# Spreading the odd layer's query products over more steps, and issuing a step's sums and normalising ahead of the next step's maxima

## The chip, the core and the metric

One core of one Trainium2 chip runs the whole program once. The metric is the device time of that launch in microseconds, the median of the runs. TensorE (PE) multiplies, ScalarE (ACT) evaluates functions and copies, VectorE (DVE) and GpSimd (POOL) do elementwise work, and SyncE (SP) issues the large loads. Each engine works through its own instructions in the order in which they were issued, and a semaphore holds an instruction until what it needs is there.

## The reference

Two layers of a diffusion trunk run over 128 context tokens and 256 latent tokens. Each layer is half a SwiGLU block, a mixer, and another half SwiGLU block. The change lies in the mixers, and mostly in that of the odd layer: windowed attention with 16 query heads, 4 key heads and one sink logit per head.

```
q = rms_norm(h @ wq); k = rms_norm(h @ wk); v = h @ wv      # q, k rotated for latent tokens
context rows:  p = softmax([q k_ctx^T, sink])               # 128 keys
latent rows:   p = softmax([q k_cache^T, q k_latent^T masked to +-128, sink])   # 384 keys
o = p[..., :-1] @ v;  out = o @ w_out
```

The even layer's mixer (differential attention beside a short convolution) runs through the same pipeline function.

## The kernel before

Activations lie transposed: 128 channels on the partitions, 384 tokens along the free axis. Every fp32 product of a weight chunk is done as three products of high and low parts (L178, L179, L180). A projection of 128 output channels is eight row chunks of three such products, summed in one PSUM tile named proj.

Tile pools give out buffers, but the order of instructions is the order in which the Python code issues them. In the odd layer odd_mixer projects keys, values and the first four heads' queries (u = 0), and then runs an attention pipeline of 24 steps. A step is a pair of heads (u, c) and one of three blocks of 128 rows: block 0 is the context rows with 128 keys, blocks 1 and 2 are latent rows with 384 keys. So steps 0, 3, 6 and so on are short, and the other two of every three are long. Below, step s is the s-th of them and block 0, 1 or 2 its kind.

The function pipeline issues, for loop counter s: a(s), the scores on PE (L1208, L1215), the maxima on DVE (L1221, L1223, L1225, L1229) and the exponentials on ACT (L1233, then L1237 for the sink); m(s-1), which adds the sink's part to the row sums and takes the reciprocal on DVE (L1241, L1242) and scales the exponentials on POOL (L1243); fill(s); b(s-3), the transposes on PE (L1253) and their copies on ACT (L1255); c(s-4), the products with the values on PE (L1266), and after a block 2 the splitting of their sum on ACT (L1273, gh) and DVE (L1274, gl); and refill, half a weight unit's splitting (L80 on ACT, L84 on DVE or POOL).

The row sums are written by the exponentials themselves, so L1241 of a step needs both L1233 and L1237 of that step. L1223 multiplies two numbers per partition with a scale that POOL has computed.

The queries of u = 1 to 3 are projected in pieces by a generator, and advance(n) takes n pieces. Eleven pieces run before the attention; fill(s) takes 1, 2, 2, 1, 1 and then 1 in each step. A piece is two row chunks. After the last piece of a chunk pair come, counted in pieces, the rotation (rope), the sums of squares over partitions (head_rows, L685) and the factors of the norm (head_rstd: transposes named cols L697 on PE, L702 on DVE, a power L189 on POOL). From step 18 on, fill also starts the output projection (products named down).

The scores, rows and cols take PSUM tiles of one tag of four buffers; proj, the transposes aT and the value products oo share four others.

Of the kernel before, what the change touches and what calls it, by code (L numbers as in the profile page):

```python
# [58 lines left out]
class Weights:  # L59
# [82 lines left out]
    def refill(self):  # L142
        self.split(self.np + self.SPLIT)
# [10 lines left out]
class Kernel:  # L154
# [637 lines left out]
    def pipeline(self, n, a, m, b, c, lag, fill, refill):  # L792

        for s in range(n + lag + 1):
            if s < n:
                a(s)
            if 0 <= s - 1 < n:
                m(s - 1)
            fill(s)
            if 0 <= s - lag < n:  # L800
                b(s - lag)
            if 0 <= s - lag - 1 < n:
                c(s - lag - 1)
            refill()
# [282 lines left out]
    def odd_mixer(self, l):  # L1087
        nc = self.nc
        okt = self.mix.tile([P, 4, 512], F32, tag="kt", name="okt")
        kt = [okt[:, i] for i in range(4)]  # L1090
        vt = [self.mix.tile([P, 512], F32, tag=f"v{i}", name=f"ov{i}")[:, 0:256] for i in range(3)] + [self.cv]
        self.cached_keys(2, okt[:, 0:2, 0:128])
        tiles = self.first_project(l, 1, AF.Exp)
        ksc = self.b3("oks")
        sqk = [self.first_squares(tiles[j], self.odd_g[:, 1:2], ksc[:, j], j) for j in range(2)]
        qs, rq = {}, {}
        qs[0] = self.mix.tile([P, 2, T], F32, tag="q", name="oq", bufs=2)
        sqq = [self.first_squares(tiles[2 + j], self.odd_g[:, 0:1], qs[0][:, j], j) for j in range(2)]
        self.w.done(2, False)
        def project(u, c):  # L1100
            if u == 2 and c == 0:
                t = self.wpool.tile([P, D], F32, tag="wp", name="oq2", bufs=1)
                qs[u] = t[:, 0:2 * T].rearrange("p (c t) -> p c t", c=2)
            elif c == 0:
                qs[u] = self.mix.tile([P, 2, T], F32, tag="q", name="oq", bufs=2)
            res = []
            yield from self.project_pieces(c, res, 2)
            sq = self.scaled_and_squares(res[0], self.odd_g[:, 0:1], qs[u][:, c], c)
            if c:
                self.w.done(1, False)  # L1110
            sqs.setdefault(u, []).append(sq)
            yield 1

        def queries():

            later = []

            def rope(u, c):
                self.rope(qs[u][:, c, TC:T], qs[u][:, c, TC:T])

            def rows(u):
                sqs[u] = self.head_rows(sqs[u])

            def rstd(u):
                rq[u] = self.head_rstd(sqs[u], f"orq{u % 2}", 0.125)

            def pieces():
                for u in range(1, 4):
                    for c in range(2):
                        yield from project(u, c)  # L1130
                        later.append([1, rope, (u, c)])
                        if c:
                            later.append([1, rows, (u,)])
                            later.append([3, rstd, (u,)])
                yield from range(3)

            for _ in pieces():
                for t in later:
                    t[0] -= 1
                    if t[0] == 0:  # L1140
                        t[1](*t[2])
                yield 1

        sqs = {}
        todo = queries()

        def advance(n):
            for _ in range(n):
                next(todo, None)

        for n, _ in enumerate(self.values(vt, 0)):
            if n == 0:
                rows = self.head_rows(sqk)
                self.w.split(self.w.np + 2)
            if n == 1:
                rk = self.head_rstd(rows, "ork", 1.0)
        rows = self.head_rows(sqq)
        advance(3)
        for j in range(2):
            self.finish_keys(ksc[:, j], rk, j, kt[j])  # L1160
        nc.scalar.dma_start(out=self.outs["odd_v"][0, 0].rearrange("t h d -> t (h d)"), in_=vt[0])

        rq[0] = self.head_rstd(rows, "orq0", 0.125)
        for j in range(2):
            nc.scalar.dma_start(out=kt[2 + j][0:64], in_=kt[j][64:128])
            nc.scalar.dma_start(out=kt[2 + j][64:128], in_=kt[j][0:64])
        for j in range(2):
            self.rope(qs[0][:, j, TC:T], qs[0][:, j, TC:T])
        advance(8)
        self.w.refill()  # L1170

        def new_keys():
            tp = self.ps("at", "nk")
            for j in range(2):
                nc.tensor.transpose(tp[:, j * P:(j + 1) * P], kt[j][:, 384:512], self.ident)
            nk = self.a2("onk")[:, 0:256]
            nc.scalar.activation(nk, tp[:, 0:256], AF.Copy)
            nc.scalar.dma_start(out=self.outs["odd_k"][0, 0].rearrange("t h d -> t (h d)"), in_=nk)

        gs = [self.g_tiles(), self.g_tiles()]  # L1180

        def fill(s):
            advance((1, 2, 2, 1, 1)[s] if s < 5 else 1)
            if s == 20:
                new_keys()
            if s == 18:
                out.append(self.out_start(gs, order, ("mm", "at", "at", "at"), 1))
            if 18 <= s < 22 or s >= 24:
                next(out[0][2], None)

        out, order = [], list(range(KC))
        self.pipeline(*self.odd_attention(qs, rq, kt, vt, gs), 3, fill, self.w.refill_half)
        self.out_projection(out[0], gs, order, self.mod_need(l, 5), (l, 2))

# [442 lines left out]
```

## Time and profile before

| | |
|---|---|
| median of 3 runs | 1518.8 us (1518.49 to 1519.86) |
| profiled execution, its own time | 1518.26 us |
| its span | 1516.5 us |
| PE busy | 1480.2 us (98%) |
| DVE busy | 1065.0 us (70%) |
| ACT busy | 654.8 us (43%) |
| POOL busy | 147.6 us (10%) |

The profile is of one execution. Its span runs from the first to the last instruction; the execution's own time is 1.76 us longer. A matmul's record overlaps the next one's, so starts are better than durations for what PE takes per product. The odd layer's attention lies at 1106 to 1203 us of the span.

### The profile page before, as it was taken

How to read it: one execution, taken by the hardware profiler on the slowest of the kernel's cores; microseconds unless marked ns; L12 is line 12 of the kernel's file. 1: busy time of each engine (PE TensorE's matmuls, PEld its weight loads, DVE VectorE, ACT ScalarE, POOL GpSimd, SP SyncE). 2: the span in 40 equal slices, each digit the busy share in tenths (PEclk: the TensorE clock that was granted, in tenths of full speed). 3: DMA queues.
4: the chain of work that ended last, by engine and by line, in shares of the span. 5: the costliest groups of instructions: out<-in, count | busy, mean ns of one | idle time of the engine just before them, and what ended most of it. 6: DMA issues, size and time to landing. Idle time of an engine off the chain costs nothing.

```text
span 1516.5 us, 22716 instructions
## 1 busy us (share of the span) xinstructions
PE 1480.2 (98%) x9082; PEld 1414.6 (93%) x9082; DVE 1065.0 (70%) x1702; ACT 654.8 (43%) x1203; POOL 147.6 (10%) x99
## 2 busy tenths in 40 slices
PE   6999999999999999999999999999998999999998
PEld 6899999999899999999999999999965799999998
DVE  3848898787777887797779868876786485434442
ACT  4632333465555543233454333324666564223331
POOL 0100000015322100000010000000454220000000
PEclk9999999999999999999999999999998999999999
DMA  9848687633323476676536656743230034433421
GB/s 348 280 155 278 202 262 246 215 117 112 108 88 116 144 232 209 202 237 213 187 105 222 223 180 214 245 165 126 86 100 29 5 112 145 134 117 127 139 91 42
DMA packets 191899, 248.61 MB, mean 164 GB/s; under 512 B 5589, under 2 KB 170034, under 8 KB 191794
## 3 DMA queue, kind: packets, MB, share of 16 engines
q1 hardware_dynamic: 190718, 245.79, 49.1%
q8 instruction: 71, 1.16, 0.3%
q10 hardware_dynamic: 1076, 1.38, 0.3%
q14 instruction: 34, 0.28, 0.1%
HBM read 244.26 MB, written 2.36 MB: 163 GB/s over the span
## 4 chain that ended last, share of the span: by engine, by line
PE 86%; DVE 7%; ACT 2%; issue 2%; POOL 1%; DMA 1%; SPq 0%; ACTq 0%; POOLq 0%; DVEq 0%
PE proj L178 18%; PE proj L180 18%; PE proj L179 18%; PE down L178 9%; PE down L179 9%; PE down L180 8%; DVE wl L84 1%; PE m_sum L237 1%; PE oo L1266 1%; DVE acc L342 1%; PE s L1208 1%; PE aT L1253 1%; DMA wm<-in_w_mod 1%; DVE x L347 1%; ACT wh L80 1%
## 5 line engine op out<-in xcount | busy, mean ns | idle before, releaser
L178 PE MATMUL proj<-xh,wh 128*128 128x384 f32 (+1 forms) x1648 | 563.1, 342 | 3.6 <-ACT bias L518 1.8
L180 PE MATMUL proj<-xh,wl 128*128 128x384 f32 (+1 forms) x1648 | 557.3, 338 | 1.1 <-DVE wl L84 1.1
L179 PE MATMUL proj<-xl,wh 128*128 128x384 f32 (+1 forms) x1648 | 556.3, 338 | 0.0
L84 DVE TENSOR_TENSOR wl<-raw,wh 128x1024 fp32r<-128x1024 f32 (+1 forms) x300 | 357.1, 1229 | 148.6 <-ACT wh L80 148.1
L80 ACT ACTIVATE wh<-raw 128x1024 fp32r<-128x1024 f32 x324 | 317.0, 1027 | 152.7 <-PE down L179 79.7
L178 PEld LDWEIGHTS proj<-xh,wh 128*128 128x128 f32 x1648 | 310.5, 188 | 18.2 <-issue 8.5
L180 PEld LDWEIGHTS proj<-xh,wl 128*128 128x128 f32 x1648 | 311.1, 189 | 1.4 <-DVE wl L84 1.4
L179 PEld LDWEIGHTS proj<-xl,wh 128*128 128x128 f32 x1648 | 310.6, 188 | 0.0
L178 PE MATMUL down<-gh,wh 128*128 128x384 f32 x832 | 280.3, 337 | 0.6 <-ACT gh L634 0.6
L179 PE MATMUL down<-gl,wh 128*128 128x384 f32 x832 | 278.8, 335 | 1.3 <-DVE gl L635 1.3
L180 PE MATMUL down<-gh,wl 128*128 128x384 f32 x832 | 278.3, 334 | 0.0
L225 DVE SCALAR_TENSOR_TENSOR macc<-wm,cpad,macc 128x1024 f32<-128x1024 f32 x210 | 259.1, 1279 | 0.1
L178 PEld LDWEIGHTS down<-gh,wh 128*128 128x128 f32 x832 | 156.3, 188 | 3.4 <-issue 2.3
L179 PEld LDWEIGHTS down<-gl,wh 128*128 128x128 f32 x832 | 156.4, 188 | 2.9 <-DVE gl L635 2.6
L180 PEld LDWEIGHTS down<-gh,wl 128*128 128x128 f32 x832 | 156.3, 188 | 0.0
L634 ACT ACTIVATE gh<-gf 128x768 fp32r<-128x768 f32 x44 | 37.2, 846 | 269.9 <-DVE gf L624 265.4
L347 DVE SCALAR_TENSOR_TENSOR x<-down,m,x 128x128 f32<-128x128 f32 x224 | 82.5, 411 | 72.5 <-PE down L180 72.5
L617 ACT ACTIVATE sg<-proj 128x384 f32<-128x384 f32 x78 | 37.9, 490 | 157.9 <-PE proj L180 157.7
L624 DVE TENSOR_TENSOR gf<-proj,sg 128x384 f32<-128x384 f32 x78 | 43.3, 555 | 79.4 <-PE proj L180 79.4
L84 POOL TENSOR_TENSOR wl<-raw,wh 128x1024 fp32r<-128x1024 f32 x24 | 61.3, 2558 | 107.3 <-ACT wh L80 95.4
L635 DVE TENSOR_TENSOR gl<-gf,gh 128x768 fp32r<-128x768 f32 x44 | 42.2, 959 | 40.1 <-ACT gh L634 40.1
L189 POOL TENSOR_TENSOR nr<-nv,neghalf 128x3 f32<-128x3 f32 x6 | 5.1, 852 | 570.6 <-DVE nv L415 570.6
(221 smaller groups left out, 1083.5 us busy)
## 6 DMA issues: line engine op xcount, KB each, us to landing
raw<-in_ffn_w SPq DMA_DIRECT2D x117, 1024.0 KB
wm<-in_w_mod SPq DMA_DIRECT2D x126, 512.0 KB
raw<-in_ffn_w SPq DMA_DIRECT2D x16, 768.0 KB
raw<-in_even_w_in SPq DMA_DIRECT2D x12, 1024.0 KB
raw<-in_odd_w_in SPq DMA_DIRECT2D x6, 1024.0 KB
raw<-in_even_w_out SPq DMA_DIRECT2D x4, 1024.0 KB
raw<-in_odd_w_out SPq DMA_DIRECT2D x4, 1024.0 KB
raw<-in_ffn_w SPq DMA_DIRECT2D x6, 512.0 KB
```

Of the source, the lines that this page charges most:

```text
L80: self.k.nc.scalar.activation(parts[0][:, a:b], raw[:, a:b], AF.Copy)
L84: engine.tensor_tensor(out=lo[:, a:b], in0=raw[:, a:b], in1=h[:, a:b].bitcast(F32), op=ALU.subtract)
L178: mm(out, w[0], x[0], start=first, stop=False)
L179: mm(out, w[0], x[1], start=False, stop=False)
L180: mm(out, w[1], x[0], start=False, stop=last)
L225: nc.vector.scalar_tensor_tensor(out=acc, in0=t, scalar=c, in1=acc, op0=ALU.mult, op1=ALU.add)
L237: self.nc.tensor.matmul(ps[32 * j:32 * j + 32, 0:256], c, v[:, j], start=first, stop=last)
L347: self.nc.vector.scalar_tensor_tensor(out=self.x[oc][:, a:b], in0=psum[:, a:b], scalar=gate[:, oc, g:g + 1], in1=self.x[oc][:, a:b], op0=A ...
L617: nc.scalar.activation(sg[c], out[:, 0:T], AF.Silu)
L624: nc.vector.tensor_tensor(out=gf[:, c], in0=out[:, 0:T], in1=sg[c], op=ALU.mult)
L634: nc.scalar.activation(gh[:, at:at + 2], gf, AF.Copy)
L635: nc.vector.tensor_tensor(out=gl[:, at:at + 2], in0=gf, in1=gh[:, at:at + 2].bitcast(F32), op=ALU.subtract)
```

## The change

In pipeline, m(s-1) is now issued ahead of a(s); this holds for both layers. In the odd layer a piece of the queries' projection is one row chunk and no longer two, all counts of pieces are doubled to keep the same place before the attention, and fill takes 2, 4, 4 pieces in the first three steps (as many row chunks as before) and then 2 and 1 in turn. Before, the chunks in steps 3 to 10 were two per step. Now there are two in odd steps and one in even ones up to step 12, and one in step 13. The sums of squares of u = 3 move from step 11 to 14 and its norm factors from step 13 to 17.

```diff
     def pipeline(self, n, a, m, b, c, lag, fill, refill):
 
         for s in range(n + lag + 1):
+            if 0 <= s - 1 < n:
+                m(s - 1)
             if s < n:
                 a(s)
-            if 0 <= s - 1 < n:
-                m(s - 1)
             fill(s)
...
             res = []
-            yield from self.project_pieces(c, res, 2)
+            yield from self.project_pieces(c, res, 1)
...
-                        later.append([1, rope, (u, c)])
+                        later.append([2, rope, (u, c)])
                         if c:
-                            later.append([1, rows, (u,)])
-                            later.append([3, rstd, (u,)])
-                yield from range(3)
+                            later.append([2, rows, (u,)])
+                            later.append([6, rstd, (u,)])
+                yield from range(6)
...
-        advance(3)
+        advance(6)
...
-        advance(8)
+        advance(16)
...
         def fill(s):
-            advance((1, 2, 2, 1, 1)[s] if s < 5 else 1)
+            advance((2, 4, 4)[s] if s < 3 else 1 + s % 2)
```

The first place is DVE in steps 7 and 8 of the odd attention. omx and ong are the maxima and their negatives, oes the sink's part, ors the row sums, gl the low half of a finished block of heads. Before:

```order
L1274 TENSOR_TENSOR gl<-oo,gh 128x384
L1221 TENSOR_REDUCE omx<-s 128x1 x2
L1223 TENSOR_TENSOR omx<-omx,orq_10291 128x2
L1225 SCALAR_TENSOR_TENSOR ong<-omx,negsink 128x2
L1229 TENSOR_TENSOR oes<-ong,negsink 128x2
L1241 TENSOR_TENSOR ors<-ors,oes 128x2
L1242 RECIPROCAL ors<-ors 128x2
```

And the same place on DVE in the changed kernel:

```order
L1274 TENSOR_TENSOR gl<-oo,gh 128x384
L1241 TENSOR_TENSOR ors<-ors,oes 128x2
L1242 RECIPROCAL ors<-ors 128x2
L1221 TENSOR_REDUCE omx<-s 128x1 x2
L1223 TENSOR_TENSOR omx<-omx,orq_10291 128x2
L1225 SCALAR_TENSOR_TENSOR ong<-omx,negsink 128x2
L1229 TENSOR_TENSOR oes<-ong,negsink 128x2
```

Both show step 7 behind the gl of step 6; L1241 and L1242 are those of step 6 in both. They stood behind the maxima of step 7 and now stand ahead of them.

The second place is PE from the scores of step 13 to those of step 14; aT and oo there are the transposes of step 10 and the value products of step 9. Before:

```order
L1208 MATMUL s<-okt,oq_10255 128x384 x2
L1215 LDWEIGHTS ident_1407
L1215 MATMUL s<-m_1409,ident_1407 128x128
L1215 LDWEIGHTS ident_1407
L1215 MATMUL s<-m_1409,ident_1407 128x128
L697 MATMUL cols<-con,rows_sb 128x64 x3
L1253 MATMUL aT<-con,e 128x128 x6
L1266 MATMUL oo<-at_sb,ov_9784 64x128 x2
L1208 MATMUL s<-okt,oq_10255 128x384 x2
```

And the same steps on PE in the changed kernel:

```order
L1208 MATMUL s<-okt,oq_10255 128x384 x2
L1215 LDWEIGHTS ident_1407
L1215 MATMUL s<-m_1409,ident_1407 128x128
L1215 LDWEIGHTS ident_1407
L1215 MATMUL s<-m_1409,ident_1407 128x128
L178 MATMUL proj<-xh,wh 128x384
L179 MATMUL proj<-xl,wh 128x384
L180 MATMUL proj<-xh,wl 128x384
L1253 MATMUL aT<-con,e 128x128 x6
L1266 MATMUL oo<-at_sb,ov_9784 64x128 x2
L1208 MATMUL s<-okt,oq_10255 128x384 x2
```

Step 13 has lost the norm factors, which now stand in step 17, and has the last row chunk of the queries, which stood in step 10.

## Rows read from the trace of the kernel before

**Rows 1.** Windows: stretch, length, busy time (instructions) by engine; PE clock, DMA, GB/s.

```profile
405.00:410.00 5.00, 5.00 (x32) 4.30 (x32) 4.13 (x11) 4.38 (x8) 0.58 (x1) 1.00 0.00 0
```

**Rows 2.** Windows of the odd attention: the same columns.

```profile
1155.00:1160.00 5.00, 2.94 (x11) 1.08 (x9) 3.10 (x9) 2.15 (x8) 4.15 (x4) 0.80 0.18 46
1160.00:1165.00 5.00, 5.00 (x33) 3.61 (x34) 2.56 (x11) 2.66 (x9) 2.95 (x2) 0.51 0.47 164
```

**Rows 3.** Waits, 1105 to 1202 us: who waited for whom, us, times, longest.

```profile
ACT e L1233 <- DVE ong L1225: 27.4, 16, 2.9
...
PEld aT L1253 <- POOL e L1243: 3.2, 3, 1.6
```

**Rows 4.** Timeline of PE: start, duration, operation, count [idle before, releaser].

```profile
1158.60 1.65 PE L1208 MATMUL s<-okt,oq 64*128 64x384 f32 x2 [2.06 <-DVE orq_v L702]
...
1185.27 0.92 PE L1208 MATMUL s<-okt,oq 64*128 64x384 f32 x4
...
1187.36 0.92 PE L1208 MATMUL s<-okt,oq 64*128 64x384 f32 x4
...
1193.20 0.38 PE L1253 MATMUL aT<-con,e 128*128 128x128 f32 x2
...
1202.37 0.61 PE L1266 MATMUL oo<-at_sb,ov 128*64 128x128 f32 x8
```

**Rows 5.** Timeline of ACT: exponentials of steps 1, 9, 22, 23; copies of step 20.

```profile
1113.23 0.67 ACT L1233 ACTIVATE e<-s,ong,orq 128x384 f32<-128x384 f32 x1 [1.89 <-DVE ong L1225]
...
1141.47 0.46 ACT L1233 ACTIVATE e<-s,ong,orq 128x128 f32<-128x128 f32 x1
...
1187.91 0.67 ACT L1233 ACTIVATE e<-s,ong,orq 128x384 f32<-128x384 f32 x1 [2.04 <-DVE ong L1225]
...
1190.06 0.68 ACT L1233 ACTIVATE e<-s,ong,orq 128x384 f32<-128x384 f32 x1
...
1191.44 0.89 ACT L1255 ACTIVATE at_sb<-aT 128x384 f32<-128x384 f32 x2
```

**Rows 6.** Timeline of DVE: maxima, sums, rotation, splitting.

```profile
1102.38 0.43 DVE L712 STREAM_SHUFFLE rope_s<-oq 128x256 f32<-128x256 f32 x1
...
1103.84 0.44 DVE L712 STREAM_SHUFFLE rope_s<-oq 128x256 f32<-128x256 f32 x1
...
1116.87 0.15 DVE L1241 TENSOR_TENSOR ors<-ors,oes 128x2 f32<-128x2 f32 x1
...
1117.14 0.47 DVE L1221 TENSOR_REDUCE omx<-s 128x1 f32<-128x128 f32 x2
1117.64 1.21 DVE L1223 TENSOR_TENSOR omx<-omx,orq 128x2 f32<-128x2 f32 x1
...
1122.12 1.22 DVE L84 TENSOR_TENSOR wl<-raw,wh 128x1024 fp32r<-128x1024 f32 x1
...
1130.78 0.16 DVE L1229 TENSOR_TENSOR oes<-ong,negsink 128x2 f32<-128x2 f32 x1
...
1143.29 0.56 DVE L1274 TENSOR_TENSOR gl<-oo,gh 128x384 fp32r<-128x384 f32 x1 [1.45 <-ACT gh L1273]
1143.77 1.01 DVE L1221 TENSOR_REDUCE omx<-s 128x1 f32<-128x384 f32 x2
...
1186.38 1.02 DVE L1221 TENSOR_REDUCE omx<-s 128x1 f32<-128x384 f32 x2
1187.44 0.16 DVE L1223 TENSOR_TENSOR omx<-omx,orq 128x2 f32<-128x2 f32 x1
...
1191.68 0.34 DVE L1241 TENSOR_TENSOR ors<-ors,oes 128x2 f32<-128x2 f32 x1 [1.32 <-ACT oes L1237]
```

**Rows 7.** Timeline of POOL: normalising of step 1, a weight's low part, a power.

```profile
1117.37 1.47 POOL L1243 TENSOR_TENSOR e<-e,ors 128x768 f32<-128x768 f32 x1 [3.01 <-DVE ors L1242]
...
1125.88 2.36 POOL L84 TENSOR_TENSOR wl<-raw,wh 128x1024 fp32r<-128x1024 f32 x1
...
1130.49 2.27 POOL L189 TENSOR_TENSOR orq<-orq_v,neghalf 128x12 f32<-128x12 f32 x1
```

## The prediction

> **What bounds the kernel now.** I read the page's shares first (in the table above): PE is busy for 98% of the span, so a change pays or costs where PE waits or runs slowly. The windows come next. In the even layer's attention PE is full (5.00 of 5 us) [rows 1], so what the new order in pipeline does there is covered. In the odd layer's attention PE falls to 2.94 of 5 us and its clock to 0.51, the lower level of 1.2 GHz [rows 2]. The clock fell behind a wait of 2.06 us, in which step 14's scores wanted the PSUM tile of the norm factors, and DVE had not read it [rows 4]. So the odd attention is the place, and there the list of waits: ACT waited 27.4 us for DVE's maxima, and PE only 3.2 us for POOL's normalising [rows 3]. A step is a loop over PE, DVE and ACT, and DVE's queue is what the exponentials wait for.
>
> Let E(s) be the start of step s's exponentials. E(1) is 1113.23 and E(22) is 1187.91, so 21 steps took 74.7 us, 3.56 each [rows 5]. PE itself needs about 2.1 us for a middle step without fill (1185.27 to 1187.36) [rows 4].
>
> **The sums ahead of the maxima.** The profile was made of the old order; here is what the new one makes of its durations. DVE now adds and inverts step s's sums before it takes the maxima of step s+1. The sums need both exponentials and the sink's. The last step shows that wait alone: L1241 starts 1.62 us after its exponentials, released by ACT's L1237 [rows 5, 6]. Before, the maxima of s+1 ran on DVE in that time; now they are queued behind the waiting instruction, then the new exponentials behind them, and DVE and ACT take turns. The turn, from E(s) to E(s+1):
>
> - L1241 after 1.62 us, and 0.27 from there to the next maxima (1116.87 to 1117.14) [rows 6].
> - The maxima of a long block to its exponentials: 1.53 us where nothing is in the way (1186.38 to 1187.91) [rows 5, 6].
> - But POOL's normalising of step s now starts with those maxima: 0.23 us after their start in the one place where the old order did the same (1117.37 after 1117.14), for 1.47 us [rows 6, 7]. In that place L1223, which takes 0.16 us at 1187.44, took 1.21 and ended with POOL's instruction [rows 6, 7]. So L1223 ends 1.71 us behind the start of the maxima, long block or short, and the exponentials come 0.31 later (1187.60 to 1187.91): 2.02 us.
>
> So a turn into block 2, or from block 2 into block 0, is 1.62 + 0.27 + 2.02 = 3.91 us. The turn from block 0 into block 1 has gl in it: gl starts 1.82 us after E (1143.29 less 1141.47), takes 0.48, the sums 0.27, the maxima 1.53, together 4.10 [rows 5, 6]. There POOL's instruction is a third as wide and I let it hide under the maxima. Three steps are 11.9 us, seven times that 83.4, against 74.7.
>
> Some turns carry more. Into step 4: no gl yet, but a rotation (1.46 us, 1102.38 to 1103.84) and DVE's part of a weight (1.22) stand ahead of the sums [rows 6], which makes 4.6 us, and a 2.36 us weight part on POOL [rows 7] can hold L1223 for 2.0 more: 0.5 to 2.5 over 4.10, and I take 2.5, as the trace has that pair of POOL instructions back to back. Into step 15 the same rotation and weight part: 1.2. Elsewhere a rotation fits beside the exponentials. Into step 18, with its scale computed only in step 17: the power (2.27 us) and the normalising behind it on POOL, 0.5. Sum 4.2, so E(22) comes 83.4 + 4.2 - 74.7 = 12.9 us later relative to E(1).
>
> At the ends: E(0) to E(1) has the same kind of collision with a weight part on POOL, 0 to 1.5, taken as 0.8. E(22) to E(23) was 2.15 and becomes 3.91: 1.8. Behind E(23), ACT ends the copies of step 20 after 2.27 us, and from the transposes of step 21 PE took 9.78 us to its last value product (1193.20 to 1202.98): 12.05, against 12.92 now [rows 4, 5]: -0.9. Sum of this edit: 12.9 + 0.8 + 1.8 - 0.9 = 14.6 us. What it gains, normalised rows earlier, is the 3.2 us of PE's waits at most [rows 3], and these lie inside steps that now wait longer for something else: nothing.
>
> The Trainium skill, in SBUF — State Buffer, section "SBUF: two separate sides", calls the port pair of VectorE and GpSimd an exclusive lock for any VectorE instruction with two SBUF inputs, as long as a GpSimd instruction that reads SBUF runs. That explains L1223, but not L1229 at 1130.78, which has two such inputs and took 0.16 us within POOL's power of 1130.49 to 1132.76 [rows 6, 7]. By the rule the power in step 17 would also hold L1241, some 1.0 us, and the sum would be 15.6; by the rows it is 14.6, and I go by the rows.
>
> **The pieces.** The chunks are only moved: 16 row chunks over steps 3 to 10 before, over steps 3 to 13 now. On PE they cost the same, and where turns last 3.9 us they lie in PE's slack (2.1 + 1.5 chunks of about 0.5 each make 2.9). The end is earlier than 17: products end in step 13, sums of squares come in 14, norm factors in 17. The 2.06 us wait of step 14 goes, since the tile of the norm factors is now asked for in step 18, with no gl and no weight part ahead of L702; but with DVE late that time is DVE's, and I count nothing for it. The weight split that follows u = 3, and its DMA on SP's queue, come three steps later; PE needs these weights only at step 18 and beyond: nothing.
>
> **The clock.** With more idle time PE can fall to 1.2 GHz more often than in the one long stretch of [rows 2]. A step's transposes, value products and scores then take some 2.4 us longer; 1.1 of it is slack, since the scores of s+1 end 2.27 + 2.4 us behind E(s-1) and are wanted 3.91 + 1.89 behind it. That is 1.3 a step, in none to six steps (14 to 17, 22, 23, which have no chunk): 0 to 8, and I take 1.5, one step's worth.
>
> **Sum.** 1518.3 (the profiled execution's own time) + 14.6 + 1.5 = 1534.4; the median of the runs is 0.5 above that execution, so 1535. The even layer adds nothing while PE is full there; if its cover went, two or three late maxima might cost up to 2 us.
>
> **Rivals.**
> *PE stays the pace-maker and the stalls go.* If DVE's sums find their exponentials done (as they do where PE is late with scores), the new order costs nothing, the wait of 2.06 and the half clock behind it (some 2.5 us lost at 0.51) go [rows 2, 4]: 1518.3 - 4.6 + 0.5, 1514. For it: ACT's waits were for DVE, and the fill is more even. Against it: the turn of 3.91 is longer than the 3.56 that a step took with fill.
> *The turns, but POOL doesn't hold L1223.* Then a turn into block 2 is 3.42 and into block 0 2.88 (maxima 0.54 shorter), three steps 10.4, seven times 72.8; with 0.5 and 1.2 for the weight parts 74.5 against 74.7, then 1.3 and -0.9 at the ends: 1519. Against it stands the row of 1.21 us, in the one place where the old order put the same instructions side by side.
> *The clock falls in all six bare steps.* 14.6 + 8 makes 1541, for PE that is busy for 2.1 of 3.9 us there, less than in the stretch that ended at 0.51 [rows 2]. Against it: each slow step fills PE, which brings the clock back.
> *That the change doesn't do what it says* is partly so: the products end at 13 and not 17; this moves nothing in the sum.
>
> **Chances.** The turns with POOL's hold, 1528 to 1539: 0.57. The clock's case: 0.18. No hold: 0.11. The faster one: 0.14. This kernel's measurement can tell about 0.2% (3 us) from no change. Faster by more: 0.13; within: 0.10; slower: 0.77, the first two cases and the no-hold case where it overshoots. The range of 1518 to 1543 leaves out the faster case and the far end of the clock's.
>
> **What would show it.** In the new profile E(1) to E(22) would be 85 to 90 us; L1223 would show about 0.6 us where the block before was a 1 and over 1.0 where it was a 2; DVE's waits for ACT's L1237 would appear in front of L1241 in most steps, with PE waiting in front of its transposes. It would be wrong if L1241 shows no waits, or if three steps take 10.7 us as before.

## The result, and the profile after

The changed kernel takes 1541.8 us (1540.5 to 1544.9, 4 runs) against 1519.3 us of the kernel before (1518.5 to 1520.0, 4 runs): a ratio of 1.0151, 95% interval 1.0136 to 1.0166. It is 22.4 us slower. The forecast was 1535, in a range of 1518 to 1543. The profiled execution took 1544.85 us, the longest of the four, with a span of 1543.1 against 1516.5 of before; 1.6 us of these 26.6 lie ahead of the even layer's attention.

The odd attention first. Waits of the changed kernel, 1105 to 1230 us (us, times, longest), which answer [rows 3]:

```profile
ACT e L1233 <- DVE ong L1225: 42.1, 21, 3.7
DVE ors L1241 <- ACT oes L1237: 22.2, 15, 1.5
PE aT L1253 <- ACT at_sb L1255: 13.1, 10, 3.3
```

DVE now waits for ACT in 15 steps, ACT for DVE in 21, and PE behind both: they take turns. ACT's timeline of the changed kernel, exponentials of steps 1, 4 and 22, against [rows 5]:

```profile
1123.67 0.67 ACT L1233 ACTIVATE e<-s,ong,orq 128x384 f32<-128x384 f32 x1 [2.27 <-DVE ong L1225]
...
1137.73 0.67 ACT L1233 ACTIVATE e<-s,ong,orq 128x384 f32<-128x384 f32 x1 [3.67 <-DVE ong L1225]
...
1213.71 0.67 ACT L1233 ACTIVATE e<-s,ong,orq 128x384 f32<-128x384 f32 x1 [2.28 <-DVE ong L1225]
```

E(1) to E(22) is 90.0 us, 74.7 before; 85 to 90 was forecast. One turn on DVE, from step 4 (E = 1137.73) into step 5 (E = 1141.64), against [rows 6]:

```profile
1139.34 0.16 DVE L1241 TENSOR_TENSOR ors<-ors,oes 128x2 f32<-128x2 f32 x1 [1.53 <-ACT oes L1237]
1139.53 0.17 DVE L1242 RECIPROCAL ors<-ors 128x2 f32<-128x2 f32 x1
1139.62 1.00 DVE L1221 TENSOR_REDUCE omx<-s 128x1 f32<-128x384 f32 x2
1140.65 0.68 DVE L1223 TENSOR_TENSOR omx<-omx,orq 128x2 f32<-128x2 f32 x1
1141.36 0.16 DVE L1225 SCALAR_TENSOR_TENSOR ong<-omx,negsink 128x2 f32<-128x2 f32 x1
```

And POOL in the same turn, against [rows 7]:

```profile
1139.84 1.47 POOL L1243 TENSOR_TENSOR e<-e,ors 128x768 f32<-128x768 f32 x1 [2.44 <-DVE ors L1242]
```

L1241 starts 1.61 us after E, the maxima 0.28 later, POOL 0.22 after them, L1223 ends with POOL's instruction and E follows: 3.91 us, as forecast. L1223 over all steps of the changed kernel, and L1241 (ns: shortest, median, longest):

```profile
L1223 DVE TENSOR_TENSOR omx<-omx,orq x24: 160/701/2174, 1119.0 to 1216.6; 128x2 f32<-128x2 f32 x24
```

```profile
L1241 DVE TENSOR_TENSOR ors<-ors,oes x24: 149/160/164, 1120.6 to 1219.3; 128x2 f32<-128x2 f32 x24
```

L1223 in the kernel before:

```profile
L1223 DVE TENSOR_TENSOR omx<-omx,orq x24: 160/161/2206, 1109.0 to 1189.5; 128x2 f32<-128x2 f32 x24
```

L1223 is held in most steps now, and was in six of 24 before. The longest turn, into step 15, took 7.00 us. On DVE:

```profile
1181.13 0.15 DVE L1241 TENSOR_TENSOR ors<-ors,oes 128x2 f32<-128x2 f32 x1
...
1181.90 1.23 DVE L1223 TENSOR_TENSOR omx<-omx,orq 128x2 f32<-128x2 f32 x1
1183.17 2.26 DVE L1225 SCALAR_TENSOR_TENSOR ong<-omx,negsink 128x2 f32<-128x2 f32 x1
```

And on POOL:

```profile
1181.65 1.47 POOL L1243 TENSOR_TENSOR e<-e,ors 128x768 f32<-128x768 f32 x1 [3.45 <-DVE ors L1242]
1183.08 2.34 POOL L84 TENSOR_TENSOR wl<-raw,wh 128x1024 fp32r<-128x1024 f32 x1
```

Behind the rotation and DVE's own weight part, L1223 waits out POOL's normalising and L1225 POOL's weight part right behind it: together 3.5 us in two instructions that take 0.16 each alone.

The clock in the odd attention, windows of the changed kernel (stretch, length, busy PE, PEld, DVE, ACT, POOL with instructions; PE clock, DMA, GB/s), against [rows 2]:

```profile
1140.00:1145.00 5.00, 5.00 (x28) 3.68 (x27) 3.29 (x10) 2.27 (x7) 2.53 (x2) 0.50 0.41 139
...
1190.00:1195.00 5.00, 4.84 (x28) 3.46 (x28) 2.35 (x8) 3.33 (x13) 2.69 (x2) 0.50 0.01 2
```

PE fell to 1.2 GHz more often than before. Around 1190 the turns into steps 16 and 17 took 4.08 and 3.94, the same as those into steps 10 and 11 at full clock, so the slow clock lay in PE's slack. Around 1145 one turn took 5.16 instead of 4.08: the value products for gl and the scores came late there, and DVE waited 0.45 us for the scores in front of the maxima.

The even layer is where the surprise was. The same view of the changed kernel there, against the full PE of [rows 1]:

```profile
420.00:425.00 5.00, 3.29 (x22) 2.76 (x21) 3.47 (x11) 2.21 (x6) 0.00 (x0) 1.00 0.65 210
425.00:430.00 5.00, 3.33 (x13) 2.05 (x13) 3.21 (x9) 2.77 (x7) 0.00 (x0) 0.90 0.00 0
430.00:435.00 5.00, 5.00 (x25) 4.96 (x24) 4.00 (x5) 2.54 (x4) 2.30 (x1) 0.76 0.00 0
```

PE's timeline there, the rows with a wait (in the kernel before there were none):

```profile
409.29 1.16 PE L1016 MATMUL o<-v,at_sb 128*128 128x128 f32 x8 [1.30 <-ACT at_sb L1008]
...
422.92 0.52 PE L1006 MATMUL aT<-con,e 128*128 128x128 f32 x3 [0.98 <-DVE y L915]
...
424.60 0.94 PE L1022 MATMUL o<-v,at_sb 128*128 128x128 f32 x6 [0.72 <-ACT at_sb L1008]
...
428.04 0.91 PE L943 MATMUL s<-kt,q 64*128 64x384 f32 x2 [1.67 <-ACT e L971]
```

Four waits, 4.67 us in all, with a fallen clock behind them (0.90 and 0.76). What lies behind the even attention comes 8.5 us later, counted from its start. Ahead of the first of these waits stands this on DVE (L989 and L992 weigh the exponentials of step 1, L961 takes the maxima of step 2):

```profile
403.20 2.23 DVE L989 TENSOR_SCALAR e<-e,rs 128x384 f32<-128x384 f32 x1
405.47 0.62 DVE L992 SCALAR_TENSOR_TENSOR e<-e,c 128x384 f32<-128x384 f32 x1
406.00 1.01 DVE L961 TENSOR_REDUCE mx<-s 128x1 f32<-128x384 f32 x2
```

And on POOL:

```profile
402.78 2.44 POOL L84 TENSOR_TENSOR wl<-raw,wh 128x1024 fp32r<-128x1024 f32 x1 [11.63 <-ACT wh L80]
```

L989 takes 0.41 us alone; here it ends some 0.2 us behind POOL's weight part. The maxima are late by that, ACT's exponentials behind them, and the copy that PE waits for stands behind the exponentials on ACT.

### The profile page after: what moved, and what is told of

Read it like the earlier page. It is cut to its first block, busy times and chain, and to the rows that moved or that the text cites. A ratio compares the mean times of both kernels' runs of the same rounds, so it can differ in the third digit from the quotient of the medians.

```text
span 1543.1 us, 22717 instructions
## 1 busy us (share of the span) xinstructions
PE 1492.2 (97%) x9082; PEld 1420.5 (92%) x9082; DVE 1073.2 (70%) x1702; ACT 654.5 (42%) x1203; POOL 148.1 (10%) x99
## 4 chain that ended last, share of the span: by engine, by line
PE 79%; DVE 9%; ACT 5%; issue 3%; POOL 2%; DMA 1%; ACTq 0%; DVEq 0%; POOLq 0%
PE proj L178 17%; PE proj L180 16%; PE proj L179 16%; PE down L179 8%; PE down L178 8%; PE down L180 8%; DVE wl L84 2%; ACT e L1233 1%; PE m_sum L237 1%; DVE omx L1223 1%; ACT wh L80 1%; DMA wm<-in_w_mod 1%; POOL wl L84 1%; DVE acc L342 1%; DVE omx L1221 1%
## 5 line engine op out<-in xcount | busy, mean ns | idle before, releaser
L347 DVE SCALAR_TENSOR_TENSOR x<-down,m,x 128x128 f32<-128x128 f32 x224 | 82.5, 411 | 72.6 <-PE down L180 72.6
```

Source lines behind the costliest of these rows:

```text
L347: self.nc.vector.scalar_tensor_tensor(out=self.x[oc][:, a:b], in0=psum[:, a:b], scalar=gate[:, oc, g:g + 1], in1=self.x[oc][:, a:b], op0=A ...
```

## The experiments

Times are medians with the ratio to the kernel before on the same chip. Where an edit adds lines, line numbers below it move on by two to six.

**The pieces alone** (both layers in the old order; the edit is against the changed kernel):

```diff
+            if s < n:
+                a(s)
             if 0 <= s - 1 < n:
                 m(s - 1)
-            if s < n:
-                a(s)
```

> The pieces alone: one row chunk long and spread as in the changed kernel, with the sums and normalising behind the next step's maxima in both layers, as before. Theory (all of the loss comes from the order in pipeline): the 2.06 us wait of step 14 goes and with it the half clock behind it, E(1) to E(22) between 70 and 75 us (before 74.7), time 1515 to 1519.5, so -0.3% to 0. Rival (the spread pieces leave PE short of work and its clock falls, which is part of the loss): 1522 to 1528, with E(1) to E(22) above 76 us.

1517.85 us, 0.9988 (0.9979 to 0.9998), E(1) to E(22) 72.6 us. A small gain. The stretch of [rows 2] is at full clock now, but the wait moved with the norm factors instead of going. PE in step 17:

```profile
1169.18 0.40 PE L697 MATMUL cols<-con,rows_sb 64*128 64x64 f32 x3 [2.03 <-DVE omx L1221]
```

The half clock followed it (0.68 in 1170 to 1175). The rival is out: the pieces are no part of the loss.

**The new order in the even layer alone**, pieces of before:

```diff
+            if lag == 2 and 0 <= s - 1 < n:
+                m(s - 1)
             if s < n:
                 a(s)
-            if 0 <= s - 1 < n:
+            if lag != 2 and 0 <= s - 1 < n:
                 m(s - 1)
```

> The new order in the even layer alone; the odd layer and its pieces as before. In the changed kernel's trace everything behind the even attention came 8.5 us later than at its start, where the prediction had put nothing. Theory (the order costs that much there by itself): 1527 to 1529, +0.55%; the odd attention's E(1) to E(22) at 74.7 us. Rival (the even layer is covered by a full PE, and the 8.5 us come from elsewhere, a start-up or a clock that varies between runs): 1519 to 1522.

1528.62 us, 1.0056 (1.0041 to 1.0071): 9.0 us, with the same four waits of PE (1.32, 0.96, 0.72, 1.67) and the odd layer as before (73.8). The loss belongs to the order in the even layer.

**The new order in the odd layer alone**, new pieces (the same edit with lag 3):

> The new order in the odd layer alone, with the changed kernel's pieces; the even layer as before. Theory (the losses of the two layers add up): odd attention from E(0) to the last gh some 108 to 111 us against 93.6, time 1532 to 1535, about +0.95%. Rival (the two layers' losses are one, for example a late start of the odd layer that moves its weight loads): under 1528 or above 1539.

1534.33 us, 1.0097 (1.0082 to 1.0112). Against the pieces alone that is 16.5 us for the order. The terms add up: -1.8 + 16.5 + 9.0 = 23.7, measured 22.4 with an interval of 20.7 to 25.2.

**Only the sum ahead of the maxima** in the odd layer; reciprocal and normalising behind them (against the run before this one):

```diff
             nc.vector.tensor_tensor(out=rs, in0=rs, in1=es, op=ALU.add)
+            return e, n, rs
+
+        def scaled(e, n, rs):
             nc.vector.reciprocal(rs, rs)
...
             if s < n:
                 a(s)
-            if lag != 3 and 0 <= s - 1 < n:
-                m(s - 1)
+            if 0 <= s - 1 < n:
+                self.rest(s - 1) if lag == 3 else m(s - 1)
```

> The kernel with the new order in the odd layer alone, but only the sum (L1241) stands ahead of the next step's maxima; the reciprocal and POOL's normalising stand behind them. So DVE still waits for the sink's exponential ahead of the maxima, but POOL's normalising starts after L1223. Theory (POOL's hold of L1223 makes 0.5 to 1.05 us of each turn): turns of 3.3 us into block 2, 2.8 into block 0, 4.0 into block 1, three steps about 10.1 us, at or under the 10.7 of before, so PE sets the pace again: E(1) to E(22) 73 to 79 us, time 1518 to 1524. Rival (the wait for the exponentials alone makes the turns, the hold lies in its shade): turns near 3.9, E(1) to E(22) above 86 us, time 1531 to 1535.

1524.31 us, 1.0034 (1.0024 to 1.0044). Its waits (the line of the sum is L1243 here), 1105 to 1230 us:

```profile
ACT e L1235 <- DVE ong L1227: 27.0, 17, 3.8
DVE ors L1243 <- ACT oes L1239: 21.2, 15, 1.5
```

And the line that was L1223:

```profile
L1225 DVE TENSOR_TENSOR omx<-omx,orq x24: 160/160/1287, 1109.3 to 1196.2; 128x2 f32<-128x2 f32 x24
```

DVE waits for the exponentials as long as without this edit (22.2 us there), and L1223 is back at 0.16. So of the odd layer's 16.5 us, 10.0 go when the reciprocal and POOL's normalising stand behind the maxima (1534.3 to 1524.3), and 6.5 stay with the sum alone ahead of them (1524.3 to 1517.85). The time and E(1) to E(22), 79.9, lie just over the upper edges of what was expected.

Neither part is one cause alone. The maxima start some 0.1 us behind the start of the sum here and 0.28 behind it with the full order, so the reciprocal made 0.2 us of a turn beside the 0.5 to 1.05 of the hold. And POOL's weight parts hold the sum itself in two turns of this run:

```profile
1126.89 1.66 DVE L1243 TENSOR_TENSOR ors<-ors,oes 128x2 f32<-128x2 f32 x1 [1.46 <-ACT oes L1239]
...
1168.58 1.82 DVE L1243 TENSOR_TENSOR ors<-ors,oes 128x2 f32<-128x2 f32 x1
```

**The new order in both layers with the pieces of before:**

```diff
-            advance((2, 4, 4)[s] if s < 3 else 1 + s % 2)
+            advance((1, 2, 2, 1, 1)[s] if s < 5 else 1)
...
-            yield from self.project_pieces(c, res, 1)
+            yield from self.project_pieces(c, res, 2)
...
```

> The new order in both layers, with the pieces of before (two row chunks long, done in step 10). Theory (where turns last 3.9 us the chunks lie in PE's slack, so the pieces are worth nothing under the new order): 1541 to 1544, the same as the changed kernel within 0.15%, though the pieces alone gave 1.8 us under the old order. Rival (the spread pieces keep PE's clock up in the bare steps also under the new order): 1545 to 1549, with more windows at the lower clock between 1155 and 1225 us.

1545.5 us, 1.0171 (1.0157 to 1.0185), against 1.0151 (1.0136 to 1.0166) with the new pieces. The time is in the rival's range, but the intervals overlap: the difference is 3.0 us, and 0 to some 6 are possible. That the pieces are worth nothing under the new order was not borne out; nothing is settled by it. In the profile the odd attention wasn't longer either (E(1) to E(22) 89.2 us, 90.0 in the changed kernel).

**The sums of the step before the last ahead of the maxima**, odd layer, new pieces:

```diff
-            if 0 <= s - 1 < n:
-                m(s - 1)
+            if lag == 3 and 0 <= s - 2 < n:
+                m(s - 2)
             if s < n:
                 a(s)
+            if lag == 2 and 0 <= s - 1 < n:
+                m(s - 1)
```

> The changed kernel's pieces, the even layer as before, and in the odd layer the sums and normalising stand ahead of the maxima, but those of the step before the last (m(s-2) ahead of a(s)). So the order on DVE is the new one, and nothing is left to wait for: the exponentials of step s-2 are done. Theory (the wait for the exponentials just issued is the root, and POOL's hold costs because that wait makes POOL start together with the maxima): no idle time in front of L1241, POOL's normalising is done before the next maxima or is hidden while PE's scores are late, E(1) to E(22) 71 to 76 us, time 1516 to 1520. Rival (sums ahead of the maxima let POOL hold L1223 whichever step they belong to): L1223 0.5 to 1.2 us in most long steps, E(1) to E(22) 78 to 86 us, time 1523 to 1530.

1524.02 us, 1.0033 (1.002 to 1.0046); E(1) to E(22) 75.8, in the theory's range, but the time is the rival's. No wait for exponentials is left, and the hold is, as DVE shows (the lines of L1241, L1223 and L1225 are L1243, L1225 and L1227 here):

```profile
1124.25 0.15 DVE L1243 TENSOR_TENSOR ors<-ors,oes 128x2 f32<-128x2 f32 x1
...
1125.56 0.68 DVE L1225 TENSOR_TENSOR omx<-omx,orq 128x2 f32<-128x2 f32 x1
1126.27 2.29 DVE L1227 SCALAR_TENSOR_TENSOR ong<-omx,negsink 128x2 f32<-128x2 f32 x1
```

Held were mostly the steps into a block 1, and the turn into step 4 (6.22 us) by POOL's weight part. So the hold doesn't need the wait: it is enough that POOL is released just ahead of the maxima.

How the two add up can be read from four profiles, from E(0) to the last gh: 91.55 us with the pieces alone, 96.24 here, 99.03 with only the sum ahead, 109.77 with the full order. Normalising ahead without the wait costs 4.7 us, the sum with its wait 7.5, both together 18.2. So they aren't two prices to be added: of the 10.7 us that the reciprocal and the normalising cost on top of the wait, under half shows without it. (The two are not quite the same work: here the rows are normalised a step later, and PE's weight loads waited 6.6 us for it, 5.0 with the pieces alone.)

**The wide part of the even layer's work behind the maxima** (new order in the even layer alone; L980 and L982 ahead, L989 and L992 behind):

```diff
+            return es, rs, n, nh, c1
+
+        def weighted(es, rs, n, nh, c1):
             maps = []
             for j in range(nh):
...
```

> The new order in the even layer alone, but only the reciprocal and the factor of lambda (L980, L982, some 0.35 us) stand ahead of the next maxima; the two wide operations on the exponentials (L989, L992, 1.0 us, and up to 2.9 where POOL's weight part holds L989) stand behind them, as before. Odd layer as before. Theory (in the even layer too it is the wait for the exponentials that makes PE late): more than half of the 9.0 us that the full order cost there stays: 1524 to 1528. Rival (the wide operations ahead of the maxima, and POOL's hold of L989, make them late): under 1522.5.

1518.92 us, 0.9997 (0.9988 to 1.0006). The whole 9.0 us are gone, and PE is full where it waited:

```profile
420.00:425.00 5.00, 5.00 (x26) 3.75 (x25) 3.27 (x8) 4.21 (x9) 0.00 (x0) 1.00 0.00 0
425.00:430.00 5.00, 5.00 (x32) 4.30 (x31) 4.38 (x9) 2.43 (x5) 2.39 (x1) 1.00 0.02 7
```

My theory fell: in the even layer the wait for the exponentials by itself costs nothing, and the loss needs the wide operations ahead of the maxima.

**POOL's weight parts in the even layer by DVE** (on the even layer's new order):

```diff
+        light, self.light = self.light, False
         self.pipeline(n, a, m, b, c, 2, fill, self.w.refill)
+        self.light = light
```

> The new order in the even layer alone (1528.6 us), and the low parts of weights that POOL splits during the even attention (some 2.4 us each) are split by DVE (1.22 us each). Theory (of the 9.0 us that the two wide operations cost ahead of the maxima, POOL's hold is the larger part: L989 took 2.23 us beside POOL's L84 where it takes 0.41 alone, twice): PE's four waits of 0.7 to 1.7 us shrink, time 1520 to 1525.5. Rival (their plain width of 1.0 us, and the 1.4 us with the reciprocal, makes the maxima late without any hold; DVE's additional parts make it later): 1527 to 1531.

1525.7 us, 1.0046 (1.0027 to 1.0066): 6.5 us of loss instead of 9.0, and PE's first waits 0.63 and 0.51 instead of 1.32 and 0.96, the last two unchanged. The time lies between the two expectations and its interval overlaps that of the even layer's new order, so what the hold costs, some 2.5 us net of DVE's additional work, isn't clear of noise; the two shorter waits show that it is there. The larger part, 6.5 us, stays without it.

**POOL's weight parts in the odd layer by DVE**, on the new order there with the new pieces:

```diff
+        light, self.light = self.light, False
         self.pipeline(*self.odd_attention(qs, rq, kt, vt, gs), 3, fill, self.w.refill_half)
+        self.light = light
```

> The new order in the odd layer alone with the changed kernel's pieces (1534.3 us), and the two low parts of weights that POOL splits during the odd attention (2.36 us each) are split by DVE (1.22 us each). Theory (in the two turns of 6.41 and 6.99 us, into steps 4 and 15, POOL's weight part right behind its normalising holds L1223 for some 2 us more): these turns become 5.2 to 5.8, E(1) to E(22) 86 to 87.5 against 88.9, time 1531 to 1533.5. Rival (these turns are long because DVE's own weight part waits for ACT's high part and the rotation, and the hold is in their shade): the turns stay over 6.3 or grow by DVE's additional 1.2 us, time 1534 to 1537.

1532.5 us, 1.0086 (1.0072 to 1.0099), E(1) to E(22) 86.2. The turns into steps 4 and 15 fell from 6.41 and 6.99 to 4.39 and 4.90, further than expected; DVE's additional part came back in the next one (5.21 into step 16). The theory holds by the turns. The gain in time, some 2 us, is not clear of noise: 1.0086 and 1.0097 have overlapping intervals.

**The same two lines in the old order with the new pieces:**

> The pieces alone under the old order (0.9988 of before), and the two low parts of weights that POOL splits during the odd attention are split by DVE. Theory (POOL's long instructions cost DVE more than they save it: in the trace of the pieces alone L1223 took 2.16, 1.11 and 0.85 us beside them, 3.6 us more than its 0.16 in three places, while the two parts cost DVE 2.4 us of a queue that has slack): the turn into step 4 falls from 4.73 to 3.5 to 4, time 1515.5 to 1517.5. Rival (DVE's queue is what the exponentials wait for, and 2.4 us more in it are late maxima): 1518 to 1521.

1518.12 us, 0.9987 (0.9978 to 0.9996), by the ratio the same as the pieces alone. The theory failed: the turn into step 4 stayed at 4.73, that into step 5 fell from 3.78 to 2.92, and those into steps 16 and 20 rose, from 4.51 to 4.95 and from 2.15 to 2.68. In sum nothing moved, for the theory or for the rival: E(1) to E(22) is 72.9 against 72.6.

**And the norm factors of u = 3 a step earlier:**

```diff
-                            later.append([6, rstd, (u,)])
+                            later.append([6 if u < 3 else 4, rstd, (u,)])
```

> The same, and the norm factors of u = 3 stand in step 16 and no longer in 17. Theory (in the trace of the pieces alone step 18's L1223 waited 0.51 us for POOL's power, and the turn into step 18 took 4.33 us): this turn becomes 3.2 to 3.9, time 0.5 to 1 us below the kernel without it. Rival (the norm factors' transposes take a score's PSUM tile where DVE reads them late, as they did in step 14 of before): PE waits for L702 ahead of the scores of step 18, time the same or 1 to 2 us above.

1518.45 us, 0.9989 (0.998 to 0.9997). The turn into step 18 went from 4.34 to 3.98, the next from 3.95 to 4.48. No gain. The new pieces in the old order stay 0.1% below the kernel before, with these last two edits or without.

## Why the prediction came out as it did

*The turns: right.* Forecast 3.91 into block 2 and into block 0, measured 3.82 to 3.94 except into steps 15 and 18; 4.10 into block 1, measured 4.06 to 4.08 in five of eight; L1223 0.6 and over 1.0, measured 0.70 and 1.2. The order's price in the odd layer, 14.6 with 1.5 for the clock, was 16.5 in the runs, and 14.7 against the kernel before, with the pieces' gain in it. The old order had a second place where POOL's normalising starts beside the maxima, which the prediction overlooked when it spoke of one: there L1223 took 1.00 us at 1140.17, which is for its reading too. One term was too small (into step 15: 1.2 forecast, 3.1 measured over 3.91, since I let POOL's second weight part hold nothing), and the 1.5 for the clock stood in for it. Into step 4, 2.5 over 4.10 was forecast and 2.3 measured. (The low end given there, 4.6 us, adds up to 4.5 from its own rows; the forecast didn't use it.)

*The even layer: wrong.* "The even layer adds nothing while PE is full there" is the step that failed, with its bound of 2 us: it cost 9.0. A full PE shows that the others are in time in the order of before. How much time they have in hand it doesn't show, and I didn't work out that the new order puts wide operations between a step's scores and its maxima, 1.0 us of them in seven turns, 2.9 where POOL holds them. The forecast of 1535 is too low by 6.8 us for that reason; with 9.0 for the even layer and -1.8 for the pieces the same sum gives 1542. That 1541.8 still lies in the stated range is luck: the range's upper end was left open for the clock, and the 1528 to 1539 given for the mechanism that showed doesn't hold it.

*The pieces at nothing:* -1.8 under the old order. That the 2.06 us wait goes was wrong there: it came back as the 2.03 of step 17.

*The clock:* its rival named 1541, which is the measured time, but not by its mechanism. PE did run at half clock in bare steps, in turns of unchanged length. Only one turn of the profiled execution grew, by 1.1 us, and in the profile of the odd layer's order alone the same turn took 4.08.

*No hold:* that rival's 1519 was too low; with L1223 freed in most steps, the sum alone ahead of the maxima in the odd layer still gives 1524.

*The rule on the port pair:* it would have held L1241 through POOL's power in step 17. POOL's power ran from 1193.78 to 1196.05 in the changed kernel, and DVE's L1241 within it:

```profile
1195.15 0.16 DVE L1241 TENSOR_TENSOR ors<-ors,oes 128x2 f32<-128x2 f32 x1 [1.45 <-ACT oes L1237]
```

It took 0.16 us, and L1241 never took over 0.164. The exclusive lock that the Trainium skill states in SBUF — State Buffer, section "SBUF: two separate sides", shows here for POOL's wide multiplications and subtractions, not for its power.

## What to carry to other kernels

An instruction put ahead of another on an in-order engine costs what it waits for, and what it releases elsewhere, and the two don't simply add: here the waiting sum alone cost 6.5 us, and the reciprocal with the POOL instruction that it releases 10.0 on top of it. Ahead of a step's critical instruction move only what is short, releases nothing that holds that step back, and finds its inputs ready or slack to wait in: short work alone cost nothing in the even layer, but 6.5 us in the odd one. And an engine that is 100% busy says that its feeders are in time, not by how much: work out their slack before pricing an edit at zero (here 9.0 us).

## What the hardware showed that was not expected

DVE's tensor_scalar with one wide input is held like those with two: L989 took 2.23 us beside POOL's weight part and 0.41 alone. As the prediction had read from one row, a multiplication of two numbers per partition is held for the rest of a POOL instruction of 1.47 us (0.70 to 1.23 instead of 0.16); the new part is that L1221, which reads PSUM, kept its 1.00 us beside the same instruction.
